# w_out as seven half-size products per pair of token tiles in a written-out order, x added by a transfer, SiLU in one ScalarE instruction

## The chip, the core and the metric

One core of a Trainium2 chip runs the program. The metric is the device time of one execution in microseconds (us). A change of under about 0.2% (2.7 us) can't be told from no change here.

## What is computed

One layer of a residual block on x of 1024 tokens by 1024 features, all in float32:

```python
def mixer(h, w_in, b_f, conv_w, w_branch, w_out):
    ...
    merged = jax.nn.sigmoid(gate_conv) * ya_d + jax.nn.sigmoid(gate_attn) * yb_d
    return jnp.einsum("bsd,de->bse", merged, w_out)

def swiglu(h, w_gate_up, w_down):
    gu = jnp.einsum("bsd,df->bsf", h, w_gate_up)
    g, u = jnp.split(gu, 2, axis=-1)
    return jnp.einsum("bsf,fd->bsd", jax.nn.silu(g) * u, w_down)

h = rmsnorm(x, norm_mix_pre[l])
m = mixer(h, w_in[l], b_f[l], conv_w[l], w_branch[l], w_out[l])
x = x + rmsnorm(m, norm_mix_post[l])
h = rmsnorm(x, norm_ffn_pre[l])
f = swiglu(h, w_gate_up[l], w_down[l])
x = x + rmsnorm(f, norm_ffn_post[l])
```

The mixer projects h by w_in (query, key, value, a short convolution's inputs and two gates), runs forgetting attention and the gated convolution, multiplies each by its half of w_branch, and adds the two under their gates: `merged`. The change is about `merged @ w_out`, the two norms behind it and the start of the feed-forward part (1024 to 2 x 2816 and back).

## The kernel before

**Precision.** Every float32 operand is cut into a high half (ScalarE copies it to the matmul's reduced format) and a low half (VectorE subtracts the copy from the source): `split`, L120. `mm3` (L125) multiplies high by high, high by low and low by high into one PSUM bank, so each block of 128x128 by 128x512 takes three matmuls.

**Strassen.** The gates and the other wide projections of w_in, gate_up and w_down go by Strassen's scheme: a 2x2 block product with seven products in place of eight. `strassen` (L626) takes the stationary sums A11, A12, S1 to S4, A22 and the moving sums B11, B21, B22, T1 to T4 (L42); each product (`prod`, L602) is 4 blocks x 3 = 12 matmuls of 512 columns, and VectorE adds the banks up to c11, c12, c21, c22. The order is A11, S2, S1, A12, S3, S4, A22. w_out does not go that way.

**Stages.** v and the first norm; the jobs of L677 (query and key, convolution, eight gates; L947), each one call of `strassen`; attention (L1235), with the convolution's branch A filled in between; branch B (L1327): for each half n of the tokens and each 128 output rows d, 12 matmuls into a bank `pbb`, then VectorE multiplies by the gate `sg` and adds into `um`, which holds `merged` transposed (8 blocks of 128 features x 1024 tokens). In the same loop w_out is read and split whole into `woh` and `wol` (L1344).

**w_out and the norms** (L1360 to L1439). For each of 8 token tiles `e_mm` splits 128 tokens of `um` and runs 2 banks x 8 blocks x 3 matmuls against `woh` and `wol`. Behind the next tile's matmuls `e_norm` (L1381) squares and sums the banks on ScalarE, takes the scale, multiplies by it and the gain row `gpo` on VectorE (scalar_tensor_tensor into `tt`), adds the tile of x that SyncE's queue has loaded (`xt`), stores the sum to `x2_dram` by GpSimd's queue, norms again with `gpr`, transposes on TensorE (8 transposes) and copies back to `um`. So `um` turns into the feed-forward input, tile by tile.

**Products ahead of gate_up.** gate_up's moving sums need all 1024 tokens, but B11 and B21 only the first 512. So `f_first` (L1415) runs A11 and A12 of the first 7 (`NPRE`) of 22 column blocks f ahead, stores both results to `pre_dram`, and the norm of the last tile and `h2_sums` (L1450, the other moving sums) run beside them. The gate_up loop (L1494) then runs five or seven products per f, and SiLU as a sigmoid on ScalarE and a multiplication by g on VectorE (L1509).

**What sets the order.** Between `strict[0] = engines` and `strict[0] = ()` the instructions of the named engines run in the order of the code; elsewhere a scheduler picks it. In `before` the stage of w_out and the norms is left to the scheduler. Every engine runs its own queue in order; transfers are issued by SyncE's queue and by GpSimd's, each in order too.

Of the kernel before, what the change touches and what calls it, by code (L numbers as in the profile page):

```python
# [38 lines left out]
NPRE = 7  # L39
# [6 lines left out]
def block_kernel(  # L46
# [100 lines left out]
    ri_dram = [dpool.tile([2, S], F32, name=f"ri_dram{j}") for j in range(4)]  # L147
    sg_dram = [dpool.tile([2, P, S], F32, name=f"sg_dram{d}") for d in range(8)]
# [306 lines left out]
    for st in range(ST):  # L455
# [20 lines left out]
        if st + 3 == ST:  # L476
            ax_close()
            w0, w0_close = pool("w0", side="right")
            r0 = w0.tile([P, KT, P], F32, name="r0")
            h0, l0 = (w0.tile([P, KT, P], F32R, name=n) for n in ("h0", "l0"))  # L480
            nc.sync.dma_start(r0, win[:, C_Q : C_Q + P].rearrange("(k p) m -> p k m", p=P))
            split(h0, l0, r0)
# [143 lines left out]
    def strassen(w, hb, psp, tmp, p1=None):  # L626
# [10 lines left out]
        add(c12, p1, b2)  # L637
# [11 lines left out]
        add(c21, p1, b2)  # L649
        return b1, c12, c21, c22  # L650

# [240 lines left out]
    def last_pair(w):  # L892

        ma, mb = (pst.tile([P, NC], F32, tag=t, name=t) for t in ("ma", "mb"))
# [52 lines left out]
    for ij, (kind, j, _, _) in enumerate(jobs):  # L947
# [35 lines left out]
        elif ij < len(jobs) - 1:  # L983
            if ij == 12:
                k_load(0)
                q_load(0)
                cb_of(0, 0)
                cb_of(0, 1)
            c11, c12, c21, c22 = strassen(pairs.get(), h1b, psm, pp)
# [52 lines left out]
    um = um_pool.tile([P, KT, S], F32, name="um")  # L1042
    yb_pool, yb_close = pool("yb", side="right")
# [3 lines left out]
    def halves_of(n):  # L1047

        return [
            tp_.tile([P, 4, NC], F32R, tag=f"y{t}{n}", name=f"y{t}{n}", bufs=1) for t in "hl"  # L1050
# [7 lines left out]
    t1, t1_close = pool("att1")  # L1058
    strict[0] = engines
# [176 lines left out]
    for t in range(2, NU + 2):  # L1236
# [33 lines left out]
        if t > NU:  # L1270
            inverse_rows(3, pss, "T", 2)()
# [22 lines left out]
    psm, psm_close = pool("psm2", 8, space=PSUM)  # L1294
# [7 lines left out]
    for _ in range(2):  # L1302
        psm.tile([P, NC], F32, tag="mm", name="pba")
# [21 lines left out]
    woh = wo_pool.tile([P, KT, D], F32R, name="woh")  # L1325
    wol = wo_pool.tile([P, KT, D], F32R, name="wol")
    for n in range(2):  # L1327
        ns = slice(n * NC, (n + 1) * NC)
        for d in range(KT):
# [14 lines left out]
            if n == 0:  # L1344
                wr = flat(raw_t())
                nc.sync.dma_start(wr, wout_d[d * P : (d + 1) * P, :])
                split(woh[:, d, :], wol[:, d, :], wr)
    tp_close()
    t0_close()


    ha_pool, ha_close = pool("ha")
    hah = ha_pool.tile([P, 2, 4, NC], F32R, name="hah")
    hal = ha_pool.tile([P, 2, 4, NC], F32R, name="hal")
    fp, fp_close = pool("f", 2)
    ep, ep_close = pool("e")
    gpo = bcast_row(norm_mix_post[0], ep, name="gpo")
    gpr = bcast_row(norm_ffn_pre[0], ep, name="gpr")

    def e_mm(st):  # L1360
        ss = slice(st * P, (st + 1) * P)
        mh, ml = hi_t(), lo_t()
        split(mh, ml, um[:, :, ss])
        pm = []
        for n in range(2):
            ns = slice(n * NC, (n + 1) * NC)
            ps = psm.tile([P, NC], F32, tag="mm", name="pm")
# [5 lines left out]
            pm.append(ps)  # L1373
        return pm

    def load_xt(st):
        xt = z_tile("xt")
        nc.sync.dma_start(xt, x2d[st * P : (st + 1) * P, :])
        return xt

    def e_norm(st, pm):  # L1381
        ss = slice(st * P, (st + 1) * P)
        xt = xts.popleft()
        if st + 1 < ST:
            xts.append(load_xt(st + 1))
        tt = ep.tile([P, D], F32, tag="t", name="tt", bufs=1)
        s2 = st_tile("s2", 2)
        for n in range(2):
            ns = slice(n * NC, (n + 1) * NC)
            nc.scalar.activation(tt[:, ns], pm[n], AF.Square, accum_out=s2[:, n : n + 1])  # L1390
        ssq = st_tile("ssq")
        add(ssq, s2[:, 0:1], s2[:, 1:2])
        rs = rms_scale(ssq)
        for n in range(2):
            ns = slice(n * NC, (n + 1) * NC)
            nc.vector.scalar_tensor_tensor(
                tt[:, ns], pm[n], rs, gpo[:, ns], op0=ALU.mult, op1=ALU.mult
            )
        add(xt, xt, tt)
        nc.gpsimd.dma_start(x2_dram[ss, :], xt)  # L1400
        ssq = st_tile("ssq")
        nc.scalar.activation(tt, xt, AF.Square, accum_out=ssq)
        rs = rms_scale(ssq)
        nc.vector.scalar_tensor_tensor(tt, xt, rs, gpr, op0=ALU.mult, op1=ALU.mult)
        for q in range(2):
            tp = psm.tile([P, 4, P], F32, tag="mm", name="tp")
            for k in range(4):
                kt = 4 * q + k
                nc.tensor.transpose(tp[:, k, :], tt[:, kt * P : (kt + 1) * P], ident)
            copy(um[:, 4 * q : 4 * q + 4, ss], tp)  # L1410
# [4 lines left out]
    def f_first(f):  # L1415
        w, _ = prep_first(f_src(f)[0])
        b1, p1 = strassen_first(w, hb, psm, fp)
        c11 = t_(fp, "c12")
        copy(c11, b1)
        nc.gpsimd.dma_start(pre_dram[f][0], p1)  # L1420
        nc.gpsimd.dma_start(pre_dram[f][1], c11)

    hb = [(hah[:, q], hal[:, q]) for q in range(2)]
    xts = deque([load_xt(0)])
    prev = None
    for st in range(ST):
        cur = e_mm(st)
        if prev is not None:
            e_norm(st - 1, prev)
        if 2 <= st < 6:  # L1430
            ss = slice((st - 2) * P, (st - 1) * P)
            for q in range(2):
                split(hb[q][0][:, :, ss], hb[q][1][:, :, ss], um[:, 4 * q : 4 * q + 4, ss])
        prev = cur
    for f in range(4):
        f_first(f)
    e_norm(ST - 1, prev)
    ep_close()
    wo_close()  # L1439

    hc_pool, hc_close = pool("hc")
    ht_pool, ht_close = pool("ht", side="right")
    hch = hc_pool.tile([P, 4, NC], F32R, name="hch")
    hcl = hc_pool.tile([P, 4, NC], F32R, name="hcl")
    hth = ht_pool.tile([P, 4, 4, NC], F32R, name="hth")
    htl = ht_pool.tile([P, 4, 4, NC], F32R, name="htl")
    hb.append((hch, hcl))
    hb += [(hth[:, b], htl[:, b]) for b in range(4)]

    def h2_sums(sl):  # L1450
# [7 lines left out]
        split(hth[:, 0:2, :, a], htl[:, 0:2, :, a], u)  # L1458
        for n, x in enumerate(((b22, b12), (b21, u[:, 1]))):
            w = t_(fp, "c22").rearrange("p (k s) -> p k s", k=4)  # L1460
            sub(w, *x)
            split(hth[:, 2 + n, :, a], htl[:, 2 + n, :, a], w)
        split(hch[:, :, a], hcl[:, :, a], b22)

    for sl in range(4):
        if 4 + sl < NPRE:
            f_first(4 + sl)
        h2_sums(sl)
# [302 lines left out]
```

## Time and profile before

| | |
|---|---|
| median of 3 runs | 1338.62 us (1338.46 to 1341.26) |
| profiled execution: its own time | 1338.93 us |
| its span, first to last instruction | 1337.2 us |
| TensorE (PE) busy | 1321.7 us, 99% of the span |
| VectorE (DVE) busy | 935.8 us, 70% |
| ScalarE (ACT) busy | 539.7 us, 40% |
| first and last w_out matmul | 602.8 and 696.2 us |
| gate_up loop and w_down on TensorE | 750.5 to 1330.5 us |

The profile has one line number, L75, for nearly everything, since a wrapper records each instruction; groups are told apart by the tiles' names (out<-in, numbers left out). `pm` are the banks of w_out, `pbb` those of branch B, `b` those of a Strassen product, `pd` those of w_down. A matmul's row gives the time from its start to the modelled end of its pipeline, so the next one starts before it ends: what a matmul costs in a row of matmuls is the distance of two starts.

### The profile page before, as it was taken

What the parts mean: (1) busy time and instruction counts of PE and PEld (TensorE: products, weight loads), DVE (VectorE), ACT (ScalarE), POOL (GpSimd) and SP (SyncE); (2) the same over time, 40 slices, a digit from 0 to 9 for tenths busy, and PEclk for the clock granted to TensorE, in tenths of its full rate; (3) what the DMA queues carried; (4) which work ended last, traced back from release to release, by engine and by line L of the source; (5) the groups of instructions that cost most, each with busy time, mean ns of one, the idle gap of its engine ahead of it and who ended that gap; (6) DMA issues with size and microseconds to landing.
All of it is one profiled execution on the core that took longest, in us unless ns stands there. A gap on an engine that the chain in (4) does not pass through costs nothing. (4 is left out here: it accounts for less than half of the span.)

```text
span 1337.2 us, 17724 instructions
## 1 busy us (share of the span) xinstructions
PE 1321.7 (99%) x6737; PEld 1096.8 (82%) x6737; DVE 935.8 (70%) x1464; ACT 539.7 (40%) x879; POOL 127.3 (10%) x252
## 2 busy tenths in 40 slices
PE   8999999999999999999999999999999999999997
PEld 7988888888887888788887888888888888888886
DVE  6983767755446867775669898677667766677585
ACT  8641322143345756524446323223222323444452
POOL 0001000010112212000002121110011101000000
PEclk9999999999999999999999999999999999999999
DMA  6342422333325445362235664332232327966441
GB/s 207 103 127 87 141 58 80 119 120 101 103 92 176 159 143 191 120 203 87 87 126 181 182 201 137 116 105 85 96 119 103 110 95 254 360 238 194 158 166 63
DMA packets 153558, 186.88 MB, mean 140 GB/s; under 512 B 9448, under 2 KB 106800, under 8 KB 153472
## 3 DMA queue, kind: packets, MB, share of 16 engines
q1 hardware_dynamic: 138736, 137.20, 32.3%
q0 software_dynamic: 14736, 48.54, 9.5%
q8 instruction: 53, 0.87, 0.3%
q14 instruction: 33, 0.27, 0.1%
HBM read 136.62 MB, written 49.09 MB: 139 GB/s over the span
## 5 line engine op out<-in xcount | busy, mean ns | idle before, releaser
L75 DVE TENSOR_TENSOR c<-c,b 128x512 f32<-128x512 f32 x195 | 133.1, 683 | 90.6 <-PE b L75 71.3
L75 DVE TENSOR_TENSOR lo<-raw,hi 128x1024 fp32r<-128x1024 f32 (+1 forms) x93 | 112.1, 1205 | 81.0 <-PE b L75 69.0
L75 ACT ACTIVATE hi<-raw 128x1024 fp32r<-128x1024 f32 (+1 forms) x100 | 101.8, 1018 | 124.3 <-PE b L75 77.2
L75 ACT ACTIVATE hi<-sx 128x1024 fp32r<-128x1024 f32 x41 | 43.6, 1063 | 238.1 <-PE b L75 210.1
L75 PE MATMUL b<-hth,lo 128*128 128x512 f32 x352 | 137.1, 389 | 0.2 <-DVE lo L75 0.2
L75 PE MATMUL b<-hth,hi 128*128 128x512 f32 x352 | 137.1, 389 | 0.1
L75 PE MATMUL b<-htl,hi 128*128 128x512 f32 x352 | 136.9, 389 | 0.0
L75 PEld LDWEIGHTS b<-hth,lo 128*128 128x128 f32 x352 | 66.1, 188 | 14.2 <-DVE lo L75 0.6
L75 PEld LDWEIGHTS b<-hth,hi 128*128 128x128 f32 x352 | 66.1, 188 | 14.1 <-DVE c L75 0.6
L75 PEld LDWEIGHTS b<-htl,hi 128*128 128x128 f32 x352 | 66.1, 188 | 13.8
L75 DVE TENSOR_TENSOR lo<-sx,hi 128x1024 fp32r<-128x1024 f32 x41 | 50.2, 1223 | 30.8 <-PE b L75 29.4
L75 PE MATMUL b<-hah,hi 128*128 128x512 f32 x176 | 68.7, 393 | 1.6 <-ACT c L75 1.6
L75 PE MATMUL b<-hal,hi 128*128 128x512 f32 x176 | 68.5, 389 | 0.0
L75 PE MATMUL b<-hah,lo 128*128 128x512 f32 x176 | 68.4, 389 | 0.0
L75 DVE TENSOR_TENSOR sx<-raw 128x512 f32<-128x512 f32 x78 | 53.7, 688 | 15.7 <-DMA raw<-in_w_in_dram 7.8
L75 PE MATMUL pd<-hi,lo 128*128 128x512 f32 x160 | 62.2, 389 | 0.0
L75 PE MATMUL pd<-hi 128*128 128x512 f32 x160 | 61.9, 390 | 0.0
L75 PE MATMUL pd<-ghi 128*128 128x512 f32 x148 | 57.6, 389 | 0.0
L75 PE MATMUL pd<-ghi,glo 128*128 128x512 f32 x148 | 57.6, 389 | 0.0
L75 PE MATMUL pd<-glo,ghi 128*128 128x512 f32 x148 | 57.6, 389 | 0.0
L75 PE MATMUL b<-hT34h,hi 128*128 128x512 f32 x136 | 53.0, 390 | 0.4 <-DVE c L75 0.4
L75 PE MATMUL b<-hT34h,lo 128*128 128x512 f32 x136 | 52.9, 389 | 0.0
(380 smaller groups left out, 3363.6 us busy)
## 6 DMA issues: line engine op xcount, KB each, us to landing
raw<-in_w_gate_up_dram SPq DMA_DIRECT2D x51, 512.0 KB, 3.7
raw<-in_w_in_dram SPq DMA_DIRECT2D x35, 512.0 KB, 3.8
a_dramS<-um POOLq DMA_DIRECT2D x44, 256.0 KB, 2.7
a_dramA<-um POOLq DMA_DIRECT2D x33, 256.0 KB, 2.7
sg<-sg_dram SPq DMA_DIRECT2D x32, 256.0 KB, 4.3
xt<-in_x_dram SPq DMA_DIRECT2D x15, 512.0 KB, 4.7
graw<-a_dramS SPq DMA_DIRECT2D x14, 512.0 KB, 3.7
sg_dram<-c POOLq DMA_DIRECT2D x24, 256.0 KB, 2.3
```

The source lines that it names most:

```text
L75: ins = getattr(self.engine, name)(*args, **kw)
```

## The change

- **w_out** runs by Strassen over pairs of token tiles: tokens 256p to 256p+255, for p = 0 to 3, are the two block rows, so a pair takes 7 products x 12 matmuls. The stationary sums come from `um` (`um_first`, `um_sums`, `um_x`, `um_2`, `um_4`), the moving sums of w_out from DRAM.
- **The moving sums of w_out** are made beside jobs 8 to 15 (convolution and gates) by `wo_steps`, called between the VectorE additions of `strassen`, and stored as high and low halves to `wt_dram` and `w22_dram`. GpSimd's queue loads them back around branch B, 1 MB each, into the places that earlier tiles leave (`w12`, `w3`, `w22`, `w4`); B11 and B21 (`w11`, `w21`) are read from w_out and split as before.
- **The norms** run per pair (`class Rows`): the scales of two tiles at once; x2 is formed by scalar_tensor_tensor, and then x is added to it by an accumulating transfer on GpSimd's queue. The second norm's row scale is a ScalarE copy, its gain a scale in ScalarE's copy out of the transposes.
- **The order** of all engines is written out from the end of branch B to gate_up, with `NPRE` 9 in place of 7 and the halves A11 and A12 of those (`f_a`, `f_b`) placed by hand among `h2_sums` and the last pair's norm.
- **SiLU** is one ScalarE instruction; VectorE's multiplication by g is gone.
- **Banks**: two PSUM banks behind attention are held by an unused tile, and branch A and B turn over six banks; `ma` and `mb` swap places.

```diff
-NPRE = 7
+NPRE = 9
...
+    def wo_steps(k):
+        both = []
+        for tag, row in (("r0", k), ("l0", k + 4)):
+            t = w0_tile(tag, F32)
+            nc.sync.dma_start(flat(t), wout_d[row * P : (row + 1) * P, :])
+            both.append(flat(t).rearrange("p (a b) -> p a b", a=2))
+        yield
+        a, b = both
+        h = flat(w0_tile("h0")).rearrange("p (a b) -> p a b", a=2)
+        copy(h[:, 0], b[:, 1])
+        strict[0] = ("vector",)
+        sub(a[:, 0], a[:, 1], a[:, 0])
+        sub(a[:, 1], b[:, 1], a[:, 1])
+        sub(h[:, 1], b[:, 1], f32(h[:, 0]))
+        for t in range(2):
+            nc.gpsimd.dma_start(w22_dram[t, k], f32(h[:, t]))
+        sub(b[:, 1], b[:, 1], a[:, 0])
+        sub(b[:, 0], b[:, 0], b[:, 1])
+        strict[0] = ()
+        for n, t in enumerate(both):
+            yield
+            h = flat(w0_tile("h0")).rearrange("p (a b) -> p a b", a=2)
+            copy(h, t)
+            strict[0] = ("vector",)
+            sub(t.bitcast(F32R), t, f32(h))
+            strict[0] = ()
+            nc.gpsimd.dma_start(wt_dram[n][0, k], f32(h))
+            nc.gpsimd.dma_start(wt_dram[n][1, k], t)
+        yield
...
-    def e_mm(st):
-        ...
-            for k in range(KT):
-                mm3(
-                    ps, (mh[:, k, :], ml[:, k, :]), (woh[:, k, ns], wol[:, k, ns]),
-                    k == 0, k == KT - 1,
-                )
-    def e_norm(st, pm):
-        ...
-        add(xt, xt, tt)
-        nc.gpsimd.dma_start(x2_dram[ss, :], xt)
...
+    class Rows:
+        def keep(self, b1):
+            copy(self.x2[0][:, n1], b1)
+            self.square(0, 0, b1, b1)
+            self.c[0, 0] = self.x2[0][:, n1]
+        def scale(self, between=None):
+            ssq = es_tile("ssq")
+            add(ssq, self.s2[:, 0:2], self.s2[:, 2:4])
+            self.rs = rms_scale(ssq, None, es_tile, 2, between)
+        def residual(self):
+            for t in range(2):
+                for n, ns in enumerate((n1, n2)):
+                    nc.vector.scalar_tensor_tensor(
+                        self.x2[t][:, ns], self.c[t, n], self.rs[:, t : t + 1],
+                        self.gpo[:, ns], op0=ALU.mult, op1=ALU.mult,
+                    )
+                nc.gpsimd.dma_start(self.x2[t], x2d[self.rows(t), :], accum_op=ALU.add)
+        def squares(self, ts=(0, 1)):
+            ...
+            for t in ts:
+                nc.gpsimd.dma_start(x2_dram[self.rows(t), :], self.x2[t])
+                self.hn.append(flat(raw_t()))
+                nc.scalar.activation(
+                    self.hn[t], self.x2[t], AF.Square, accum_out=self.ssq[:, t : t + 1]
+                )
...
+    for p in range(4):
+        ...
+        prod(b1, w["A11"], wob[B11], True)
+        copy(p1, b1)
+        ...
+        prod(b2, w["S2"], wob[T2], True)
+        if prev:
+            prev.residual()
+        add(c12, p1, b2)
+        ...
+        prod(b3, w["S1"], wob[T1], True)
+        add(c22, p1, b3)
+        ...
+        prod(b1, w["A12"], wob[B21], False)
+        if prev:
+            prev.squares()
+        ...
+        prod(b2, w["S3"], wob[T3], False)
+        if not more:
+            low_b = hb_split(1)
+        if prev:
+            prev.normed(lambda: add(c22, c22, b2))()
+        else:
+            add(c22, c22, b2)
+        ...
+        prod(b3, w["S4"], wob[B22], False)
+        add(c12, c12, b3)
+        here.square(0, 1, c12)
+        prod(b2, w["A22"], wob[T4], False)
+        add(p1, p1, b2)
+        here.square(1, 0, p1)
+        here.scale(low2)
+        if prev:
+            prev.turn()
+        here.load_g()
...
+    f_load(2)
+    f_load(3)
+    f_a(0)
+    prev.residual()
+    f_split(2)
+    f_a(1)
+    sums = h2_sums(0)
+    ...
+    f_b(3)
+    prev.turn()
...
-            nc.scalar.activation(sg, g, AF.Sigmoid)
-            mul(sg, sg, g)
+            nc.scalar.activation(sg, g, AF.Silu)
             mul(yf[:, ns], sg, u)
```

Three places in the engines' queues show what moves. On GpSimd's queue, before, nothing stands between attention's mask additions (`cb`) and the first stores of x2; the numbers behind a name are those of the buffer.

```order
L75 DMA sg_dram_134<-c_3339 128x512
L75 TENSOR_TENSOR cb<-cb,mask 128x128 x2
L75 DMA sg_dram_134<-c_3338 128x512
L75 TENSOR_TENSOR cb<-cb,mask 128x128 x58
L75 DMA x_dram<-xt 128x1024 x7
```

Now the ten loads of w_out's sums stand there (`w12`: T2, then T1; `wl_5702` and `wh_5701`: T3; `wl_5879` and `wh_5878`: T4; `w22`: B22), and behind them the first pair's two accumulating transfers (`x<-in_x_dram`).

```order
L75 DMA w12h<-wt_dram_130 128x4x512
L75 DMA w12l<-wt_dram_130 128x4x512
L75 DMA w12h<-wt_dram_129 128x4x512
L75 DMA w12l<-wt_dram_129 128x4x512
L75 DMA wl_5702<-wt_dram_129 128x4x512
L75 DMA wh_5701<-wt_dram_129 128x4x512
L75 DMA wl_5879<-wt_dram_130 128x4x512
L75 DMA w22h<-w_dram 128x4x512
L75 DMA w22l<-w_dram 128x4x512
L75 DMA wh_5878<-wt_dram_130 128x4x512
L75 DMA x_5978<-in_x_dram 128x1024
L75 DMA x_5979<-in_x_dram 128x1024
```

What moved: 10 MB of loads now stand between attention and the norm, and each store of x2 stands behind a transfer that adds x. The last four loads wait for places that branch B still uses: T4's for `yh1` and `yl1`, which TensorE reads to the last `pbb` matmul, `w22` for the `sg` tiles, which VectorE reads last. On ScalarE, before, one token tile's norm reads like this (`hah`: a half of B11 or B21).

```order
L75 ACTIVATE tt,s_5975<-pm 128x512 x2
L75 ACTIVATE hah<-um 128x4x128
L75 ACTIVATE sq<-va 128x1
L75 ACTIVATE hah<-um 128x4x128
L75 ACTIVATE tt,ssq<-xt 128x1024
L75 ACTIVATE sq<-va 128x1
L75 ACTIVATE hi<-um 128x1024
L75 ACTIVATE um<-tp 128x4x128 x2
```

Now pair 1 reads like this on ScalarE: behind the squares of `x_5978` and `x_5979`, which the accumulating transfers complete, stand the second norm of pair 0 (`raw`) and then pair 1's own squares and the high half of pair 2 (`hi<-um`).

```order
L75 ACTIVATE raw,ssq<-x_5978 128x1024
L75 ACTIVATE raw,ssq<-x_5979 128x1024
L75 ACTIVATE sq<-va 128x2
L75 ACTIVATE raw<-x_5978,r_6139 128x1024
L75 ACTIVATE raw<-x_5979,r_6139 128x1024
L75 ACTIVATE x_6147<-b_6032 128x512
L75 ACTIVATE b_6032,s_6149<-b_6032 128x512
L75 ACTIVATE x_6148,s_6149<-c_6037 128x512
L75 ACTIVATE hi<-um 128x1024
L75 ACTIVATE x_6147,s_6149<-c_6036 128x512
L75 ACTIVATE x_6148,s_6149<-c_6035 128x512
L75 ACTIVATE sq<-va 128x2
```

So whatever holds up the first two rows holds up everything of the next pair's norm. On VectorE, `c_6036`, `c_6037` and `c_6035` are pair 1's c12, c22 and c21; the addition of bank S3 into c22 now stands behind `va`, which needs those two squares.

```order
L75 SCALAR_TENSOR_TENSOR x_5979<-c_5895,r_6025,raw 128x512
L75 TENSOR_TENSOR c_6036<-c_6035,b_6033 128x512
L75 TENSOR_TENSOR sx<-um 128x512
L75 TENSOR_TENSOR um<-um 128x4x128
L75 TENSOR_TENSOR sx<-um 128x512
L75 TENSOR_TENSOR s_6080<-um,sx 128x512
L75 TENSOR_TENSOR c_6037<-c_6035,b_6034 128x512
L75 TENSOR_TENSOR s4l<-s_6080,s4h 128x512
L75 TENSOR_TENSOR lo<-um,hi 128x1024
L75 TENSOR_SCALAR va<-ssq 128x2
L75 TENSOR_TENSOR c_6037<-c_6037,b_6033 128x512
```

TensorE's last product of a pair (A22) writes the bank that this last row reads.

More of the change, by code (lines that the diff above doesn't have):

```diff
@@ L1343, in block_kernel @@
             add(um[:, d, ns], um[:, d, ns], sg)
[L1344 to L1347, printed above, removed]
+            if n == 0 and d < 4:
+                op, half = (w11, w21)[d // 2], slice(d % 2 * 2, d % 2 * 2 + 2)
+                split(
+                    op[0][:, half], op[1][:, half],
+                    load_wo(d * 2, n1),
+                )
+        if n == 0:
+            w3 = halves_of(0, "w")
+            load_sum(w3, 0, 1)
@@ L1442, in block_kernel, with both_hi_lo, hb_split, low @@
[L1442 to L1448, printed above, removed]
+    def both_hi_lo():
+        return hi_t(), lo_t()
+    hb = []
+    def hb_split(n):
+        op = wide_op(wo_pool, ("w11", "w21")[n])
+        hb.append(op)
+        lows = [
+            halves(*(t[:, k : k + 2] for t in op), um[:, 4 * n + k : 4 * n + k + 2, n1])
+            for k in (0, 2)
+        ]
+        def low():
+            for x in lows:
+                x()
+        return low
```

380 lines of the change are left out of this document (288 added, 92 removed).

## The prediction

> **What bounds the kernel now.** I read the page's head first, then who waited for whom on TensorE, then the chain that ends last in order of time, then the groups and windows of the stages that the change touches. Head of the page, two rows of TensorE's waits (engine and tile, releaser: us in total, times, longest), two of the chain (start us, us, what):
>
> ```profile
> span 1337.2 us, 17724 instructions
> PE 1321.7 (99%) x6737; PEld 1096.8 (82%) x6737; DVE 935.8 (70%) x1464; ACT 539.7 (40%) x879; POOL 127.3 (10%) x252
> ...
> PE b L75 <- ACT c L75: 1.6, 1, 1.6
> ...
> PE tp L75 <- DVE tt L75: 0.3, 1, 0.3
> ...
> 750.53 370.24 PE b L75 x1632
> 1120.76 209.70 PE pd L75 x924
> ```
>
> TensorE is the bound nearly everywhere. The last 580 us of the chain are matmuls without a gap, and the two waits shown are the only ones over 0.2 us between branch B and gate_up: 1.9 us to be had from better order there, no more. So only fewer matmuls can shorten the kernel by much, and any new wait of TensorE lengthens it by as much.
>
> A matmul's price is the distance of two starts: 370.24 / 1632 = 0.2269 us (w_down: 209.70 / 924 = 0.2269). The 389 ns of a row below is the time to the modelled end and would make the gain 1.7 times too large. A product of 12 matmuls takes 2.72 us. w_out in the group view by tile (count: min/median/max ns, first and last start):
>
> ```profile
> L75 PE MATMUL pm<-woh,hi x128: 389/389/477, 602.8 to 695.7; 128*128 128x512 f32 x128
> L75 PE MATMUL pm<-wol,hi x128: 389/389/397, 603.1 to 696.0; 128*128 128x512 f32 x128
> L75 PE MATMUL pm<-woh,lo x128: 388/389/398, 603.3 to 696.2; 128*128 128x512 f32 x128
> ```
>
> **Removed.** 3 x 128 = 384 matmuls become 4 pairs x 7 x 12 = 336: 48 x 0.2269 = **10.9 us**, all on the path. Transposes stay 64. `NPRE` 9 moves products ahead of gate_up and removes none. With the waits above, 10.9 + 1.9 = 12.8 us is the most that can go.
>
> **SiLU.** VectorE loses 44 multiplications (30 us), and TensorE gets nothing for it. Two groups (count | busy us, mean ns | idle before), then gate_up as a window (length, then PE, PEld, DVE, ACT, POOL busy, clock, DMA share, GB/s):
>
> ```profile
> L75 DVE TENSOR_TENSOR sgf<-sgf,c 128x512 f32<-128x512 f32 x29 | 19.9, 686 | 3.5 <-ACT sgf L75 3.0
> L75 DVE TENSOR_TENSOR sgf<-sgf,b 128x512 f32<-128x512 f32 x15 | 10.3, 688 | 2.7 <-ACT sgf L75 2.7
> ...
> 750.53:1120.76 370.23, 370.23 (x1633) 306.67 (x1634) 277.07 (x387) 105.49 (x135) 44.51 (x82) 1.00 0.36 120
> ```
>
> TensorE fills that window already: zero. ScalarE is at 28%, so SiLU could take twice a sigmoid's time and stay hidden.
>
> **w_out's sums beside the gates.** Per pair of jobs (38 us of TensorE) five subtractions of 512 columns and two of 1024, 5 x 0.69 + 2 x 1.22 = 5.9 us on VectorE, some 2.7 us on ScalarE, 2.5 MB stored and 1 MB loaded. A window in the gates:
>
> ```profile
> 300.00:320.00 20.00, 20.00 (x90) 16.56 (x89) 10.04 (x13) 6.57 (x9) 2.17 (x4) 1.00 0.40 126
> ```
>
> VectorE goes from 10 to 13 of 20 us, and each step stands behind an addition whose successor is due 5 us later. The new loads on SyncE's queue and stores on GpSimd's each have most of a job's time. Zero; without that cover, 5.9 us per two jobs.
>
> **Loads around branch B.** Ten transfers of 1 MB. Six have tens of us. The last four (T4 low, B22 high and low, T4 high) can start only when branch B ends. Two branch B windows, then the last `sg` product and sum on VectorE:
>
> ```profile
> 570.00:580.00 10.00, 10.00 (x46) 8.29 (x45) 8.86 (x12) 4.98 (x6) 0.00 (x0) 1.00 0.86 304
> 580.00:590.00 10.00, 10.00 (x46) 8.29 (x45) 6.93 (x10) 0.93 (x1) 0.00 (x0) 1.00 0.85 277
> ...
> 604.13 0.68 DVE L75 TENSOR_TENSOR sg<-sg,pbb 128x512 f32<-128x512 f32 x1
> 604.73 1.22 DVE L75 TENSOR_TENSOR lo<-um,hi 128x1024 fp32r<-128x1024 f32 x1
> 605.87 0.68 DVE L75 TENSOR_TENSOR um<-um,sg 128x512 f32<-128x512 f32 x1
> ```
>
> 304 / 0.86 gives some 340 GB/s when the engines are full, 3.1 us per MB. T4 low starts at 602.8, B22 high at about 606.5, the others behind it. `c<-pre_dram` (below) lands 256 KB in 3.3 us, 0.8 of it bytes, so 2.5 us are fixed: B22 high lands at 612.1, B22 low at 615.2, T4 high at 618.3. S4, the first to need B22, starts at 602.8 + 5 x 2.72 = 616.4, A22 at 619.2. Zero, with about 1 us to spare; the other end is half that rate (rival B).
>
> **The norm's loop.** This decides. Clock 0 is the start of a pair's first product; a pair lasts 7 x 2.72 + 1.6 (16 transposes, below: 8 take 34.23 - 33.44 = 0.79) = 20.7 us; the first pair has no transposes behind it. Durations:
>
> ```profile
> 33.44 1.03 PE L75 MATMUL tp<-ident,hn 128*128 128x128 f32 x8
> 34.23 0.37 PE L75 MATMUL pv<-wvh,hB11h 128*128 128x260 f32 x1
> ...
> L75 DVE SCALAR_TENSOR_TENSOR tt<-pm,r,gpo 128x512 f32<-128x512 f32 x16 | 11.3, 746 | 0.7
> L75 DVE TENSOR_TENSOR lo<-um,hi 128x1024 fp32r<-128x1024 f32 x8 | 9.7, 1222 | 8.4 <-PE pm L75 8.2
> L75 DVE RECIPROCAL r<-sq 128x1 f32<-128x1 f32 x16 | 2.6, 162 | 3.7 <-ACT sq L75 3.7
> ...
> L75 ACT ACT_TABLE_LOAD x11 | 14.1, 1283 | 4.1 <-DMA x_dram<-xt 1.9 <-DVE s L75 1.4 <-PEq L1752 0.7
> L75 ACT ACTIVATE tt<-pm 128x512 f32<-128x512 f32 x16 | 9.4, 603 | 3.8 <-PE pm L75 3.8
> L75 ACT ACTIVATE tt<-xt 128x1024 f32<-128x1024 f32 x8 | 8.5, 1060 | 27.4 <-DVE xt L75 27.3
> L75 ACT ACTIVATE hi<-um 128x1024 fp32r<-128x1024 f32 x8 | 8.1, 1054 | 14.8 <-PE pm L75 11.0 <-PE pbb L75 3.8
> L75 ACT ACTIVATE sq<-va 128x1 f32<-128x1 f32 (+1 forms) x24 | 5.1, 211 | 4.0 <-DVE va L75 4.0
> ...
> 602.83:697.23 94.40, 94.07 (x441) 77.39 (x440) 60.06 (x130) 40.14 (x87) 3.77 (x7) 1.00 0.30 101
> ```
>
> Pair 1: VectorE's last addition of pair 0 0.7, its square 0.8 with the sum's readout, a table load for the square root 1.3 (the scheduler put the warm-up ahead of the last sigmoid), the root 0.2 and five or six VectorE steps of some 0.2 on two columns, 1.3 together, four scalar_tensor_tensor 2.9: the second accumulating transfer starts at 7.0 and lands at 7.0 + L. Behind it the square 1.24, `va` 0.15 and the addition into c22 0.68, all due before A22 at 6 x 2.72 = 16.3: **L up to 7.2 us is free.** From pair to pair the loop closes through ScalarE's fixed order: L + 1.24 (square) + 1.9 (scale, with the c22 addition) + 1.9 (two copies) + 3.8 (pair's copy, squares, high half) + 5.4 (scale, low half 1.22, scalar_tensor_tensor) = L + 14.2 against 20.7: **above L = 6.5 it falls behind.** Pair 3 has two more copies (1.9) between square and root; its transposes are due at 19.05 and come at 7.0 + L + 7.0, so L = 6.2 costs 1.1 us there.
>
> The trace has no accumulating transfer. Nearest rows (KB each, us to landing):
>
> ```profile
> xt<-in_x_dram SPq DMA_DIRECT2D x15, 512.0 KB, 4.7
> ...
> cb<-c_dram SPq DMA_DIRECT2D x10, 512.0 KB, 6.2
> ...
> x_dram<-xt POOLq DMA_DIRECT2D x8, 512.0 KB, 2.9
> ...
> c<-pre_dram POOLq DMA_DIRECT2D x14, 256.0 KB, 3.3
> ...
> tk<-in_w_down_dram SPq DMA_DIRECT2D x5, 512.0 KB, 12.6
> ```
>
> It reads the same x tile (4.7) and besides reads and writes the tile in place; load and store one after the other would be 7.6. The ends are 2.9, the plain store, and 12.6, the slowest landing of 512 KB. I take 6.2, between 4.7 and 7.6: 1.1 us.
>
> **Ahead of gate_up.** 18 products and 16 transposes, 50.6 us of TensorE; VectorE needs for the other moving sums 4 x 6.0, seven low halves 8.5, the norm 4 and the first f's sums 5.8, some 43 us: it fits. The last pair's gain row is loaded only when pair 2's transposes leave its place; at 4.7 to 6.2 us for such a load (`xt` and `cb` above), four scalar_tensor_tensor 2.9 and a low half 1.2 the third column block's operand is ready 8.8 to 10.3 us in, 0.2 to 1.7 after its turn. I take 0.8.
>
> **Sum**, from the profiled execution's 1338.9 (0.3 over the runs' median): - 10.9 - 1.9 + 1.1 + 0.8 = **1328.0 us**. With nothing new waiting it is 1326.1; with L at 7 and the gain row late, 1331: that is the forecast's own span.
>
> **Rivals.** A: *the accumulating transfer is slow.* At L = 7.6 the stalls add up to 4.7 us (pair 1 0.4, pairs 2 and 3 1.1 each, pair 3's transposes 2.1): 1332. At 9.4 (twice 4.7) 10.3 us: 1337. The gain is gone near L = 10; at 12.6 the A22 waits are 5.4, 6.1 and 6.1, the transposes 2.1 and 3.4, 23.1 us: **1349, slower.** For it: two reads and a write per element, two transfers 1.4 us apart on the same engines. Against: the DMA engines were 0.30 busy in this stage (the window above), and the store of the same size lands in 2.9.
>
> B: *w_out's last four loads come late.* At half the rate (6.2 us per MB) B22 low lands at 623.9 and T4 high at 630.1: S4 waits 7.3 us, A22 3.7, together 11.0: **1339**, no gain. At 250 GB/s it is 2 us or so. Against it stand the two windows; for it, that they are mostly SyncE's transfers in larger pieces. The Trainium skill ("DMA: Bandwidth & Descriptors", section Bandwidth) lists 6.15 us for a 1 MB load issued from GpSimd; by that alone B would come true, whereas the trace's store of 512 KB from GpSimd, 2.9 us, speaks for a better rate.
>
> C: *the written-out order is late elsewhere*: a low half or a copy behind a waiting instruction on VectorE or ScalarE, a few us in the part ahead of gate_up: 3 to 6 us, 1331 to 1334. For it: VectorE's 43 of 50.6 us there leave little room for a wait ahead of a full queue.
>
> **How the numbers follow.** Forecast 0.57; A from 1331 to 1338 0.09, above 1338 0.10; B 0.12, half of it near no gain; C 0.12. Range 1325 to 1337.5: nearly all of the forecast and of C, most of A's lower part, two thirds of B, 0.83. Under 1336.2: 0.57 + 0.12 + 0.07 + 0.06 = 0.82; within 0.2%: 0.09; slower: 0.09.
>
> **What would show it.** 48 fewer matmuls of 512 columns, no TensorE wait on a weight tile (`w22`, `wh`, `wl`) and none over 2 us between branch B and gate_up. L near 6 in the transfers' list. A: TensorE's A22 waits for VectorE's c, ScalarE's squares wait for the transfer. B: TensorE waits for `w22` once, at the first pair's S4. C: a wait for `lo`, `hi` or `raw` ahead of gate_up. I am wrong if TensorE waits beside the gates or in gate_up.

## The result: 0.7% slower

The changed kernel takes 1349.4 us (median of 4 runs, 1348.0 to 1351.4) against 1339.9 of the kernel before (4 runs, 1338.5 to 1341.3): a ratio of 1.0072, with a 95% interval of 1.0052 to 1.0091. The forecast was 1328.0, with 1325 to 1337.5 around it: a gain of 10.9 us was forecast, and 9.4 us were lost. The profiled execution took 1349.8 us.

The head of the changed kernel's page:

```profile
span 1348.0 us, 17768 instructions
PE 1316.8 (98%) x6689; PEld 1089.3 (81%) x6689; DVE 927.9 (69%) x1432; ACT 570.8 (42%) x921; POOL 160.1 (12%) x302
```

Who waited for whom on TensorE, without the rows of the first stages (us in total, times, longest):

```profile
PE b L75 <- DVE c L75: 8.5, 8, 2.8
PE b L75 <- DMA w22l<-w_dram: 4.6, 1, 4.6
...
PE b L75 <- DMA wh<-wt_dram: 1.5, 1, 1.5
PE b L75 <- DVE lo L75: 1.4, 3, 0.5
...
PE tp L75 <- ACT raw L75: 1.1, 2, 0.7
PE b L75 <- ACT c L75: 1.0, 1, 1.0
PE pd L75 <- ACT hi L75: 0.9, 1, 0.9
...
PE b L75 <- ACT hi L75: 0.4, 1, 0.4
```

TensorE has 6689 matmuls instead of 6737, the 48 fewer that were counted on. It also has some 19 us of waits where there were 1.9, in every row that the prediction had named as the sign of a rival: `w22` and `wh` (B), VectorE's c and the transposes (A), `lo`, `hi` and ScalarE's c ahead of gate_up (C).

From w_out's first matmul to w_down's first, before took 517.8 us (602.83 to 1120.60) and the changed kernel 526.5 (603.32 to 1129.86). The removed matmuls take 10.9 away, so 19.7 us were lost elsewhere. Sorted by place, as the excess of each distance between two starts over 0.2269 us (before has 3.3 us of such excess in all, and the remaining 0.8 us are in distances too small to list):

| place | us | forecast |
|---|---|---|
| first pair's S4, waiting for `w22` and `wh` | 8.0 | 0 |
| A22 of pairs 1 to 3, waiting for VectorE's c | 6.1 | 0 |
| transposes | 2.1 | 1.1 |
| ahead of gate_up and at its start | 6.0 | 0.8 |
| outside: w_out starts 0.5 later, w_down takes 1.65 longer | 2.1 | 0 |

From the profiled execution of before: 1338.9 - 10.9 + 19.7 + 2.1 = 1349.8.

**The first pair's S4.** TensorE's rows, then GpSimd's issues (start, length, and in brackets the time since its last instruction):

```profile
616.92 0.39 PE L75 MATMUL b<-w22h,s4h 128*128 128x512 f32 x1
621.86 0.80 PE L75 MATMUL b<-w22l,s4h 128*128 128x512 f32 x1 [4.55 <-DMA w22l<-w_dram]
622.45 0.63 PE L75 MATMUL b<-w22h,s4l 128*128 128x512 f32 x1
622.88 0.63 PE L75 MATMUL b<-w22h,s4h 128*128 128x512 f32 x1
...
625.68 0.39 PE L75 MATMUL b<-w22h,s4l 128*128 128x512 f32 x1
627.59 0.47 PE L75 MATMUL b<-wh,hi 128*128 128x512 f32 x1 [1.52 <-DMA wh<-wt_dram]
```

```profile
603.66 0.76 POOL L75 DMA_DIRECT2D wl<-wt_dram  x1 [11.40 <-PE pbb L75]
609.41 0.75 POOL L75 DMA_DIRECT2D w22h<-w_dram  x1 [4.99 <-issue]
615.42 0.76 POOL L75 DMA_DIRECT2D w22l<-w_dram  x1 [5.26 <-issue]
622.12 0.75 POOL L75 DMA_DIRECT2D wh<-wt_dram  x1 [5.94 <-issue]
```

S4 starts at 616.9, where the forecast had it (616.4). Its operand's low half lands 5 us later, and S4 takes 10.7 us instead of 2.7. The four loads are issued 5.8, 6.0 and 6.7 us apart, though nothing that the profile shows holds GpSimd. The one before has landed 0.3 us earlier each time: at 609.1, 615.1 and 621.8.

Behind the wait the matmuls stand 0.43 us apart for 3 us; in the window 621.86 to 624.98 the granted clock is 0.51, which costs 1.5 us more. The Trainium skill ("TensorE: Matmul & The Clock Gate", section Part 1: The HAM clock gate (the "warmup" mystery)) puts TensorE at half clock after some 3.4 us without work. This trace agrees: half clock behind 4.55 us, and behind the 2.83 us of the next rows only one distance of 0.34. Other runs don't: `layout` (below) fell to half clock behind a wait of 2.81 us, and `sp_loads` kept its clock behind 3.13. So the length of a wait alone doesn't decide it here.

**A22 in pair 1.** GpSimd's two accumulating transfers, ScalarE's square of the second, VectorE's `va` and the addition that stands behind it, TensorE:

```profile
636.34 0.93 POOL L75 DMA_DIRECT2D x<-in_x_dram  x1 [13.47 <-DVE x L75]
637.70 0.86 POOL L75 DMA_DIRECT2D x<-in_x_dram  x1 [0.43 <-DVE x L75]
...
647.72 1.06 ACT L75 ACTIVATE raw<-x 128x1024 f32<-128x1024 f32 x1 [3.78 <-DMA x<-in_x_dram]
...
648.90 0.17 DVE L75 TENSOR_SCALAR va<-ssq 128x2 f32<-128x2 f32 x1 [4.14 <-ACT raw L75]
648.98 0.69 DVE L75 TENSOR_TENSOR c<-c,b 128x512 f32<-128x512 f32 x1
...
649.72 0.50 PE L75 MATMUL b<-wh,hi 128*128 128x512 f32 x1 [2.83 <-DVE c L75]
```

The second transfer starts 7.4 us into the pair (forecast 7.0) and lands 10.0 us later; in pairs 2 and 3 it takes 9.0 and 6.9. The steps from there to A22 have the lengths that the prediction gave them.

### The profile page after: what moved, and what is told of

Its sections match the earlier page's. It is cut to its first block, busy times and chain, and to the rows that moved or that the text cites. A ratio compares the mean times of both kernels' runs of the same rounds, so it can differ in the third digit from the quotient of the medians.

```text
span 1348.0 us, 17768 instructions
## 1 busy us (share of the span) xinstructions
PE 1316.8 (98%) x6689; PEld 1089.3 (81%) x6689; DVE 927.9 (69%) x1432; ACT 570.8 (42%) x921; POOL 160.1 (12%) x302
## 4 chain that ended last, share of the span: by engine, by line
PE 73%; issue 13%; DMA 5%; DVE 4%; ACT 2%; POOL 2%; SPq 0%; POOLq 0%; DVEq 0%; ACTq 0%
PE b L75 42%; PE pd L75 16%; PE pba L75 3%; PE po L75 3%; PE tps L75 3%; PE pv L75 3%; DMA x<-in_x_dram 3%; PE sp L75 2%; PE ma L75 1%; DVE lo L75 1%; DMA raw<-in_w_gate_up_dram 1%; PE mb L75 1%; DVE c L75 0%; DVE sx L75 0%; ACT hi L75 0%
## 5 line engine op out<-in xcount | busy, mean ns | idle before, releaser
L75 DVE TENSOR_TENSOR c<-c,b 128x512 f32<-128x512 f32 x215 | 146.7, 683 | 95.1 <-PE b L75 84.8
L75 PE MATMUL b<-w12h,lo 128*128 128x512 f32 x208 | 80.9, 389 | 0.0
L75 PE MATMUL b<-w12h,hi 128*128 128x512 f32 x204 | 79.4, 389 | 0.0
L75 PE MATMUL b<-w12l,hi 128*128 128x512 f32 x204 | 79.4, 389 | 0.0
L75 PE MATMUL b<-hh,hi 128*128 128x512 f32 x176 | 68.7, 390 | 1.3 <-DVE c L75 1.3
L75 PE MATMUL b<-hh,lo 128*128 128x512 f32 x176 | 68.5, 389 | 0.0
L75 PE MATMUL b<-hl,hi 128*128 128x512 f32 x176 | 68.5, 389 | 0.0
L75 POOL DMA_DIRECT2D a_dramA<-um x33 | 18.0, 545 | 298.6 <-DVE um L75 298.0
L75 PE MATMUL b<-hT34l,hi 128*128 128x512 f32 x136 | 52.9, 389 | 0.0
L75 PE MATMUL b<-hT12h,hi 128*128 128x512 f32 x136 | 52.9, 389 | 0.0
```

The costliest lines, as they stand in the source:

```text
L75: ins = getattr(self.engine, name)(*args, **kw)
```

## The experiments

**Theory.** The prediction's arithmetic of engines is right, and two transfers on GpSimd's queue are not what it took them for. (1) The queue takes one 1 MB load of 512 pieces at a time. (2) An accumulating transfer keeps the DMA engines busy much longer than a plain one. Rivals: the memory or the engines are simply full; the order on VectorE is at fault; VectorE has no room.

Each run but `best2` and `best3` is a single execution. Beside these runs the kernel before took 1338.0 to 1342.7 us, so what a run says of 3 us or less is read from its trace and not from its time.

### Where the late loads come from

`sp_loads`, the ten loads on SyncE's queue:

```diff
-            nc.gpsimd.dma_start(f32(o), wt_dram[n][t, :, :, x, :].rearrange("k p c -> p k c"))
+            nc.sync.dma_start(f32(o), wt_dram[n][t, :, :, x, :].rearrange("k p c -> p k c"))
```

(and the same for `w22`)

> The ten 1 MB loads of w_out's sums go through SyncE's queue instead of GpSimd's; nothing else is changed. Theory (GpSimd's queue takes one such load at a time, some 6 us each): on SyncE's queue the last four overlap, land within about 12 us of branch B's end, the first pair's S4 no longer waits (before this: 4.6 + 1.5 us and seven matmuls at half clock, 8.0 us in all), and the time is 1340 to 1342 against the changed kernel's 1349.4. Rival (the DMA engines or the memory are what is full): the loads take as long on either queue, S4 and A22 wait 5 us or more in sum, 1348 to 1350.

`layout`, GpSimd's queue again, but larger pieces:

```diff
-    wt_dram = [dpool.tile([2, 4, P, 2, NC], F32, name=f"wt_dram{n}") for n in range(2)]
-    w22_dram = dpool.tile([2, 4, P, NC], F32, name="w22_dram")
+    wt_dram = [dpool.tile([2, 2, P, 4, NC], F32, name=f"wt_dram{n}") for n in range(2)]
+    w22_dram = dpool.tile([2, P, 4, NC], F32, name="w22_dram")
...
-            nc.gpsimd.dma_start(wt_dram[n][0, k], f32(h))
+            nc.gpsimd.dma_start(wt_dram[n][0, :, :, k].rearrange("x p c -> p x c"), f32(h))
...
-            nc.gpsimd.dma_start(f32(o), wt_dram[n][t, :, :, x, :].rearrange("k p c -> p k c"))
+            nc.gpsimd.dma_start(f32(o), wt_dram[n][t, x])
```

> The same ten loads stay on GpSimd's queue, but the intermediate arrays in memory are laid out so that a load has 128 pieces of 8 KB instead of 512 of 2 KB (the stores beside the gates get twice as many pieces of half the size). Theory that the queue is full by the number of pieces, not by bytes: several loads are under way together, issues follow each other in under 3 us, S4 waits under 1 us, 1340 to 1342. Rival (one load at a time whatever its pieces, or a rate of the queue): issues stay 6 us apart, S4 waits 4 us or more, 1348 to 1350.

Measured: 1341.7 and 1341.5 us; no wait for `w22` or `wh` is left in either. On SyncE's queue the last three loads, still of 512 pieces, are issued 0.4 and 0.6 us apart. The last four issues of `layout`:

```profile
603.41 0.53 POOL L75 DMA_DIRECT2D wl<-wt_dram  x1 [20.64 <-PE pbb L75]
606.47 0.53 POOL L75 DMA_DIRECT2D w22h<-w_dram  x1 [2.53 <-DVE um L75]
607.26 0.53 POOL L75 DMA_DIRECT2D w22l<-w_dram  x1 [0.27 <-issue]
607.86 0.53 POOL L75 DMA_DIRECT2D wh<-wt_dram  x1
```

The DMA engines in 40 slices (GB/s), the changed kernel from 603 to 628 us and `layout` from 603 to 620:

```profile
GB/s 26 0 0 79 105 387 419 419 269 0 0 0 85 66 184 419 419 413 92 131 367 282 157 85 203 413 380 380 98 20 0 0 33 72 282 413 419 419 39 0
```

```profile
GB/s 0 0 0 116 193 77 289 443 443 405 463 154 135 347 405 347 463 366 482 424 405 443 405 443 443 366 482 405 424 424 231 164 251 280 231 135 19 0 0 0
```

The changed kernel's four bursts reach 413 to 419 GB/s and have empty slices between most of them; with a quarter as many pieces, of four times the size, the same queue moves the same bytes without a gap. So the memory isn't full and GpSimd's queue isn't slow. What the pieces change is how many loads the queue has under way. Why is not shown; room for descriptors, the records that tell an engine what to move, is an inference. The Trainium skill ("DMA: Bandwidth & Descriptors", section SWDGE vs HWDGE vs iDMA) says that GpSimd writes a transfer's descriptors into a ring in SBUF which the DMA engines drain. The kernel sets `dynamic_dma_scratch_size=1024`; a larger reserve wasn't tried.

From w_out to w_down, `layout` takes 518.1 us instead of 526.5: late loads cost 8.4 us. `layout` itself lost 1.5 us more to a half clock behind pair 1's A22 wait. The wait, and the window behind it (length, PE, PEld, DVE, ACT, POOL busy, clock, DMA share, GB/s):

```profile
641.40 0.50 PE L75 MATMUL b<-wh,hi 128*128 128x512 f32 x1 [2.81 <-DVE c L75]
...
642.04:645.40 3.36, 3.36 (x10) 2.63 (x9) 1.89 (x3) 3.09 (x5) 0.00 (x0) 0.52 0.04 13
```

### Where the accumulating transfer's time comes from

`no_acc`, the same transfers without adding (the residual sum then lacks w_out's part):

```diff
-                nc.gpsimd.dma_start(self.x2[t], x2d[self.rows(t), :], accum_op=ALU.add)
+                nc.gpsimd.dma_start(self.x2[t], x2d[self.rows(t), :])
```

> The eight transfers that add x become plain loads of x over the same tile, at the same place and on the same queue; the residual sum then lacks w_out's part. Theory (adding in the transfer is what takes 7 to 10 us): the plain load lands in about 4.7 us, A22 waits less than 0.5 us in all, the transposes do not wait, 1342 to 1344. Rival (the queue or the neighbours' traffic make it slow, adding costs little): 6.5 us or more to landing, waits of 4 us or more remain, 1347 to 1350.

Measured: 1339.6, faster than the theory's range, though the wait for `w22` is still in it (5.3 us). There is no A22 wait in the pairs and no wait of the transposes. The second transfer of pair 1 lands in 6.5 us instead of 10.0. The transfers' list, changed kernel and `no_acc` (KB each, median us to landing):

```profile
x<-in_x_dram POOLq DMA_DIRECT2D x8, 512.0 KB, 6.9
```

```profile
x<-in_x_dram POOLq DMA_DIRECT2D x8, 512.0 KB, 4.8
```

`c22_first`, the addition ahead of `va`:

```diff
-            prev.normed(lambda: add(c22, c22, b2))()
+            add(c22, c22, b2)
+            prev.normed()()
```

> VectorE's addition of S3's bank into c22 is put ahead of the norm's first step va (in the pairs behind the first), so that A22's bank comes free without the accumulating transfer; all else as in the changed kernel. Theory (the transfer is late and the addition only stands behind it in VectorE's order): the three waits of A22 for VectorE's c, 5.7 us, go to under 0.5; the transposes wait as before or up to 0.7 us longer for each pair; 1343.5 to 1345.5. Rival (the norm's loop is longer than a pair, so that what A22 doesn't wait for the transposes or the next pair's operands do): the waits move, 1348 to 1350.

Measured: 1347.4, just under the rival's range. TensorE's waits, the three longest in sum:

```profile
PE tp L75 <- ACT raw L75: 5.3, 5, 1.9
PE b L75 <- DMA w22l<-w_dram: 4.3, 1, 4.3
PE b L75 <- DVE c L75: 2.5, 4, 1.1
```

The A22 waits are gone (of the 2.5 us of c, 1.8 are at gate_up's start and 0.7 in the first stages), and the transposes now wait 5.3 us instead of 1.1. The rival holds: the loop from pair to pair is longer than a pair, as the prediction worked out for L above 6.5, and the order on VectorE only decides where TensorE pays.

`quiet`, on top of `layout`: both stores of the residual rows behind both transfers, the gain row on GpSimd's queue behind them:

```diff
-                nc.gpsimd.dma_start(x2_dram[self.rows(t), :], self.x2[t])
                 self.hn.append(flat(raw_t()))
...
+        def store(self):
+            for t in range(2):
+                nc.gpsimd.dma_start(x2_dram[self.rows(t), :], self.x2[t])
+
         def normed(self, between=None):
+            self.store()
...
-            nc.sync.dma_start(self.gpo, norm_mix_post[0].partition_broadcast(P))
+            nc.gpsimd.dma_start(self.gpo, norm_mix_post[0].partition_broadcast(P))
```

> On top of the pieces of 8 KB (1341.5): while two accumulating transfers are under way nothing else of this stage uses the DMA engines. The two stores of the residual rows go out behind both transfers, and the gain row (512 KB) is loaded on GpSimd's queue behind them. Theory (the 10.0, 9.0 and 6.9 us of the second transfer are mostly shared engines): it lands in 6.5 to 7.5 us in all pairs, the three A22 waits fall from 5.7 us to under 1.5, 1336 to 1338. Rival (adding in the transfer is slow by itself): 8 us or more in pairs 1 and 2, waits over 4 us, 1340 to 1342.

Measured: 1342.4, slower than either side expected; the second transfer takes 7.9, 7.9 and 6.8 us, and the A22 waits are 0.8, 1.3 and 0.3 us. In `layout` it took 9.9, 8.8 and 6.8, so sharing with other traffic was 2.0 us in pair 1 and 0.9 in pair 2. What is left is the two accumulating transfers themselves, against a median of 4.8 for plain ones in `no_acc`. The DMA engines between 630 and 634, when little else than the two accumulating transfers uses them:

```profile
DMA packets 174, 0.65 MB, mean 162 GB/s; under 512 B 16, under 2 KB 16, under 8 KB 174
...
q0 software_dynamic: 174, 0.65, 92.2%
```

They move 162 GB/s at 92% busy, against 419 for a plain load: at that rate the 1 MB of a pair takes some 6.5 us. The gain in the pairs was lost again: the last pair's gain row, now behind the stores, came late, and TensorE waited 1.8 us for a low half at 701.5.

### Adding x on VectorE, and what is left

`vec_add`, on top of `layout`:

```diff
+        def load_x(self):
+            for t in range(2):
+                nc.sync.dma_start(self.x2[t], x2d[self.rows(t), :])
...
+                    c = self.c[t, n]
                     nc.vector.scalar_tensor_tensor(
-                        self.x2[t][:, ns], self.c[t, n], self.rs[:, t : t + 1],
+                        c, c, self.rs[:, t : t + 1],
                         self.gpo[:, ns], op0=ALU.mult, op1=ALU.mult,
                     )
-                nc.gpsimd.dma_start(self.x2[t], x2d[self.rows(t), :], accum_op=ALU.add)
+                    add(self.x2[t][:, ns], self.x2[t][:, ns], c)
```

> On top of the pieces of 8 KB (1341.5): x is loaded plainly by SyncE into the residual tile half a pair ahead, the scaled rows are made in place, and VectorE adds them (8 additions of 512 columns in place of 2 transfers' adding, 16 more instructions in all, 2.7 us for each pair); the squares' unused results go to a bank. Theory (the accumulating transfer alone is what A is): no A22 wait, no wait of the transposes, what is left ahead of gate_up is 2 to 4 us, 1331 to 1333.5. Rival (VectorE, 14 of 21 us busy in a pair, becomes the late one): waits for c or lo in the pairs, 1335 to 1339.

Measured: 1338.6. The A22 waits are 0.2 us in pairs 1 and 2, but ahead of gate_up and at its start TensorE waits 7.1 us, against 4.6 in `layout`. Its rows of c and lo over the whole run:

```profile
PE b L75 <- DVE c L75: 4.2, 9, 1.0
PE b L75 <- DVE lo L75: 3.5, 4, 1.9
```

The number is the rival's, the place is not: VectorE has room in the pairs, none behind the last. There its eight instructions (four scalings, four additions) stand ahead of the third f's low half, for which TensorE waits 1.9 us.

`layout_no_acc` (both edits above together) asks what the two transfers cost without anything in their place:

> Pieces of 8 KB and, with them, plain loads of x in place of the accumulating transfers (the residual sum lacks w_out's part). Theory (the late loads of w_out's sums and the accumulating transfer are separate costs, and VectorE's added instructions explain why adding on VectorE gave back only 3 us): both go, the time is 1330.5 to 1332.5, and what is left over the forecast's 1328 are the waits ahead of gate_up, 3 to 5 us. Rival (they overlap: a first pair that ends earlier only runs into the next lateness): 1336 to 1338.5, near the 1338.6 of the kernel that adds on VectorE.

Measured: 1333.0, near the theory. From w_out to w_down it takes 508.4 us; the forecast's own terms give 517.8 - 10.9 - 1.9 + 1.1 + 0.8 = 506.9. The costs are separate, and they add up: 526.5 - 508.4 = 18.1 us, where `layout` alone gives 8.4 and `no_acc` alone (517.2 us) 9.3.

`best1`, on top of `vec_add`: one table load for the square root, and the last pair's gain row in a free tile:

```diff
                 nc.scalar.activation(sg, sg, AF.Sigmoid)
+                if n:
+                    nc.scalar.activation(warm, sg[:, 0:1], AF.Sqrt)
...
-    nc.scalar.activation(warm, ones[:, 0:1], AF.Sqrt)
...
+        here.load_g(None if more else hi_t())
```

> The kernel with x added by VectorE, with two edits more: the warm-up of the square root reads the last sigmoid's result, so that its table is loaded once and before the pairs (1.28 us less on ScalarE in pair 1), and the last pair's gain row is loaded into a free tile half a pair earlier. Theory (what is left ahead of gate_up is lateness handed on from the last pair): the waits for lo and c ahead of gate_up fall to under 1.5 us, 1329.5 to 1331.5. Rival (ScalarE's copies, which now wait for the first f's products to leave their tile, cost as much): 1331.5 to 1334.

Measured: 1338.1. Both ranges missed: the gain row was not what the third f's low half waited for (still 1.7 us, behind the last pair's eight instructions).

`npre7`, on top of `layout`: `NPRE = 7`, without the steps of f 7 and 8.

> On top of the pieces of 8 KB (1341.5): seven products pairs (f 0 to 6) are moved ahead of gate_up as in the kernel before, not nine; four products, two loads and four stores less stand there. Theory (the 2.4 us of waits for c at gate_up's start come from weights that land late because the DMA engines are 0.79 busy with the loads and stores of the moved products): those waits fall under 1 us, 1339 to 1340.5. Rival (the moved products are the time that VectorE needs for the moving sums): waits for hh, w12 or w22 appear, 1342 to 1345.

Measured: 1346.9, the rival's side and beyond its number. The waits for c at gate_up's start only gave way to another of TensorE's waits:

```profile
PE b L75 <- ACT hi L75: 5.5, 1, 5.5
```

The four products more ahead of gate_up are cover for the operands of its first f: VectorE makes their sums behind the last of the other moving sums. Whether the moved products' own traffic made gate_up's start late can't be told from this run.

`sigm`, on top of `layout`: SiLU undone.

```diff
-            nc.scalar.activation(sg, g, AF.Silu)
+            nc.scalar.activation(sg, g, AF.Sigmoid)
+            mul(sg, sg, g)
```

> On top of the pieces of 8 KB (1341.5): SiLU is undone, so ScalarE makes a sigmoid and VectorE multiplies by the gate, 44 multiplications more on VectorE (30 us). Theory (TensorE fills gate_up either way): gate_up takes 359.4 us from its first to its last matmul within 0.5, the time is within 1.5 us of 1341.5. Rival (SiLU's place on ScalarE gave VectorE the room that it needs): additions into c come late, 2 us or more slower.

Measured: 1339.9, 1.6 us under `layout`, which one execution can't tell from nothing. The same 356 us of gate_up as a window (length, then PE, PEld, DVE, ACT, POOL busy), `layout` and `sigm`:

```profile
763.00:1119.00 356.00, 356.00 (x1572) 294.76 (x1571) 244.58 (x339) 101.14 (x129) 46.64 (x86) 1.00 0.38 125
```

```profile
763.00:1119.00 356.00, 356.00 (x1572) 294.78 (x1571) 271.09 (x380) 101.28 (x129) 46.64 (x86) 1.00 0.38 125
```

26.5 us less on VectorE, 1572 matmuls in both: SiLU is worth nothing.

### A version that beats both

`best2`, on top of `vec_add`: the accumulating transfer kept for the last pair, where two products cover it; `c22_first`; one table load; and the seventh f's high half behind the copy that TensorE waits for:

```diff
-                    add(self.x2[t][:, ns], self.x2[t][:, ns], c)
+                    if self.p < 3:
+                        add(o, o, c)
+                if self.p == 3:
+                    nc.gpsimd.dma_start(self.x2[t], x2d[self.rows(t), :], accum_op=ALU.add)
...
-    low_6 = f_halves(6)
     f_load(7)
-    low_6()
     sums = h2_sums(2)
     f_a(4)
+    low_6 = f_halves(6)
```

> A version meant to beat both: pieces of 8 KB; x added by VectorE in the first three pairs, by the accumulating transfer in the last, where two products lie between it and its reader; the addition into c22 ahead of va; the square root's table loaded once; the high half of the seventh f's operand made behind the copy of the fifth f's first product. Theory (each wait left in the kernel with x on VectorE has its cause in the order named): the 1.8 us at the third f's lo, the 1.2 us at ScalarE's c and most of the A22 waits go, 1333 to 1335.5 against 1338 to 1340 before, a ratio of 0.996 or so. Rival (VectorE and the DMA engines are full ahead of gate_up, so waits only move): 1336.5 to 1339.

Measured: 1333.9 us, 0.996 of before (0.9942 to 0.9978). The waits for ScalarE's c and for the third f's low half are gone, each with the order that had been named for it; w_out to w_down takes 510.7 us.

`best3`, on top of `best2`, takes up w_down's start:

```diff
-    gfo = bcast_row(norm_ffn_post[0], gp, name="gfo")
-    tk = [gp.tile([P, 2, NC], F32, name=f"tk{g}") for g in range(NG)]
     tl = [gp.tile([P, 2, NC], F32, name=f"tl{g}") for g in range(NG)]
+    gfo = bcast_row(norm_ffn_post[0], gp, name="gfo")
+    tk = [gp.tile([P, 2, NC], F32, name=f"tk{g}") for g in range(NG)]
```

> The version meant to beat both (1333.9), with w_down's two sets of column tiles allocated the other way round, so that the gain row and the first three weight tiles (tk) come to lie where the last f of gate_up is done earlier. Theory (w_down's start is 1 to 2 us late in every run of the changed kernel because SyncE issues the gain row and tk only when the last f's S4 product frees the place, 2.5 us ahead of w_down's first matmul against 3.5 before): they are issued 3.5 us or more ahead, TensorE's wait for hi at w_down's start goes, 1332.5 to 1333.5. Rival (SyncE stands behind the loads ahead of them in its queue, or the transfer itself is slow at this point): the wait stays at 0.5 to 1.6 us, 1333.5 to 1335.5.

Measured: 1333.0 us, 0.9955 of before (0.9939 to 0.9972), too near `best2` to tell the medians apart. The traces do tell: SyncE's issue of the gain row, changed kernel (w_down's first matmul at 1129.86) and `best3` (1111.63):

```profile
1127.33 0.35 SPq L75 DMA_DIRECT2D gfo<-in_norm_ffn_post_dram  x1
```

```profile
1108.16 0.41 SPq L75 DMA_DIRECT2D gfo<-in_norm_ffn_post_dram  x1
```

2.5 us ahead became 3.5, TensorE's wait for `hi` is gone, and w_down takes 209.6 us, as before (209.5; 211.1 in the changed kernel). In the changed kernel this issue waits for the last S4 product of gate_up on TensorE, and in before and `best3` it does not: the change had moved w_down's first tiles to a place that is freed later.

## Why the prediction was wrong

- **Removed**: right. 48 matmuls fewer, 10.9 us.
- **SiLU**: right, zero, shown by `sigm`.
- **w_out's sums beside the gates**: right within 0.5 us, by which w_out starts later.
- **Loads around branch B**: this step failed. It let the four loads follow each other at the engines' rate behind a fixed part and called for 612.1, 615.2 and 618.3. The rate was even underrated (340 GB/s taken, 419 measured) and the deadlines were right; but one load at a time is on its way, 5.8 to 6.7 us from issue to issue, and `w22l` landed at 621.8, `wh` at 627.5. Rival B had the landings (623.9 and 630.1 at 6.2 us per MB) and their price (11.0 for 8.0) nearly right, but for the reason "half the rate", which the bursts of 419 GB/s disprove: that it came so near is luck. The prediction's evidence against B was windows of other transfers in other pieces, from another queue. The Trainium skill's 6.15 us for such a load ("DMA: Bandwidth & Descriptors", section Bandwidth) was the better guide to the times from issue to landing here, 5.3 to 6.4 us. The Trainium skill gives it as the time that the engines are busy. There it differs, and the trace decides: 1 MB at 419 GB/s is a burst of 2.5 us.
- **The norm's loop**: this step failed in one size, L. All else held: the second transfer starts at 7.4 us (7.0 was written, though the terms add up to 7.2), the loop falls behind once L is over its limit (`c22_first` shows that it does), and with L of 10.0, 9.0 and 6.9 rival A's model, 10.3 us at 9.4 throughout, stands against 8.2 measured at A22 and the transposes. L was set to 6.2 between two plain transfers. Adding moves bytes at 0.4 of a plain load's rate (162 of 419 GB/s), which no row of before could tell; sharing makes up the rest (`quiet`). The upper end of 12.6 was in the text, its chance was too small.
- **Ahead of gate_up**: this step failed too. 0.8 was taken, 6.0 measured, 4.7 of them still there when both transfers are cured (the sum of the excesses in `layout_no_acc`). VectorE's sum "43 of 50.6 us" was no proof that it fits: the waits are those of one instruction behind another in a fixed order, and `best2` took some of them out by order alone. What holds up the others stays open.
- **The chances.** A, B and C were priced one by one; each alone, at the size that it turned out to have, would have left the time at 1336 or under. All three came at once. A and B hang on the same unknown, how GpSimd's transfers behave (though `layout` and `no_acc` show two separate causes), so a case with both should have stood in the range: 1328 + 11.0 + 9.2 + some 4 of C = 1352.
- Left out altogether: w_down's start, 1.65 us, since no instruction of it was changed; the place of its tiles was.

## What to carry to other kernels

Price a transfer three times: by its bytes at the engines' rate, by its fixed part, and by how many of its kind the queue will hold. When the trace of before has none of that kind from that queue in those pieces, each of its consumers is a rival, and several can come true together, as here. Large contiguous pieces for what one core stores for itself to load again cost nothing that these runs show, and were worth 8 us here. Adding inside a transfer saves VectorE's instructions, but belongs where nobody waits for the sum within 10 us.

## What the runs showed of the hardware

- GpSimd's queue: 1 MB loads of 512 pieces go out 5.8 to 6.7 us apart, each 0.3 us after the one before has landed; with 128 pieces of 8 KB three go out within 1.4 us and move at some 420 GB/s (`layout`). On SyncE's queue loads of 512 pieces go out 0.4 and 0.6 us apart (`sp_loads`).
- An accumulating transfer of 512 KB from memory into SBUF: 6.9 us in the median and 10.0 at most, two at a time; plain 4.8 and 6.5 (`no_acc`). In the pairs its issue takes GpSimd 0.86 to 0.93 us, the plain one's 0.53 to 0.57.
- TensorE's granted clock fell to 0.51 for 3.1 us behind a wait of 4.55 us (changed kernel), to 0.52 for 3.4 us behind 2.81 us (`layout`), and to 0.55 for 2.4 us soon after two waits of 1.9 and 0.7 us with one transpose between them (`c22_first`). It stayed at 1.00 behind 2.83 us (changed kernel) and 3.13 us (`sp_loads`). What decides is not shown.
